# A hybrid decoder block on one core: six split FFN groups, half of SH2 on VectorE, low parts made for two chunks at once

## The chip, the cores and the metric

The kernel runs on one core of one Trainium2 chip. The metric is the device time of one execution in microseconds; a median of several runs stands for a kernel, and one further execution is profiled.

## The reference

One decoder block over 256 tokens of width 2048, all in float32. From a conditioning vector come six vectors (adaLN: shift, scale and gate for each of two halves).

```
mod = silu(c) @ w_ada + b_ada                      # w_ada: 2048 x 12288
sh1, sc1, g1, sh2, sc2, g2 = split(mod, 6)
h = rms_norm(x) * (1 + sc1) + sh1
q, k, v, gb, gc, xt = split(h @ w_in, ...)         # w_in: 2048 x 6144
attn = attention(rms_norm(q), rms_norm(k), v)      # 8 heads of 128, causal
conv = gb * causal_dwconv(gc * xt)                 # 3 taps
x = x + g1 * (concat(rms_norm(attn), rms_norm(conv)) @ w_out)
h2 = rms_norm(x) * (1 + sc2) + sh2
u_gate, u_up = split(causal_dwconv(h2 @ w_ffn_up), 2)   # w_ffn_up: 2048 x 11264
x = x + g2 * ((silu(u_gate) * u_up) @ w_ffn_down)       # w_ffn_down: 5632 x 2048
```

With 256 tokens there is a single attention block, so the selection of past blocks selects nothing.

## The kernel before, in words

**Matmuls in two parts.** TensorE multiplies float32 values that are split in a high part (rounded to the fast format) and a low part (the rest). Each weight tile (128 x 4 x 512) is loaded into a buffer `raw`, ScalarE writes the high part (`split_hi`, L242), VectorE the low part (`split_lo`, L248), and then the next load may start. Activations are split in the same way: a *chunk* is 128 of the 2048 channels for 256 tokens, transposed, with its high half in columns 0 to 255 of a tile and its low half behind. High times high, high times low and low times high are summed in PSUM.

**Slots.** The whole program is one list of slots, written out by hand and by the numbers in `CFG`. A slot uses one weight tile (1 MB; down-projection tiles can be smaller). Slots 0 to 47 are the input projection, in the order of `turns`; slots 48 to 63 the output projection; from slot 64 on come the FFN's segments (`segs`: 8, 5, 5 and 4 groups of 256 gate and 256 up channels), each up-projection followed by its share of the down-projection. While slot i multiplies, the weights of slot i + 2 are split (`la` is 2). All other work is a task put at a slot by `at(...)`; `cls` says whether it stands before (under 2) or behind (2) the split in program order. Each engine runs its instructions in this order. `x_first` and `hi_late` choose, slot by slot, whether the split comes early or late.

**Loads** are issued by SyncE in the order in which they are used, five buffers deep. Each waits until the tile five before it has been used up.

**adaLN.** w_ada is 96 further tiles of 1 MB, fed in between the slots. An entry of `ada` is a piece: part (0 SH1, 1 SC1, 2 G1, 3 SH2, 4 SC2, 5 G2), first chunk, width, whether TensorE sums it, first slot, and how many slots its tiles are spread over. A VectorE piece multiplies each row block by its value of silu(c) and adds (L299). A TensorE piece does the same with matmuls of 32 columns (L293) that hold one PSUM bank until `evac`. `cols` then transposes the sum into columns (L337) and gets A and B, the scale and shift of a chunk; `h_chunks` and `h2_chunks` make the modulated chunks from these, `spread` broadcasts a gate. `fill` is one more TensorE piece, whose tiles lie around `norm2`, the norm between the halves, where TensorE would wait.

**The input projection.** A turn is a tensor (or a pair such as q0, q1) and a range of chunks. Two turns of the same tensor at most two slots apart go on in the same PSUM banks; otherwise `evac_in` empties the banks, the first time with a ScalarE copy (L420), later with a VectorE add (L422). There are eight banks; a pair's turn uses four.

**FFN.** A group takes 4 weight tiles (16 chunks) and 4 banks. In segment 0 the first five groups are done in two turns (`split`: 5 groups, cut at chunk 8): chunks 0 to 7 for all five, then chunks 8 to 15, since the last chunks' scale and shift come late. Each turn ends in `up_sum` (L633, L636; the second adds to the first, L641). `up_conv`, `up_silu` and `up_gate` (L650 to L669) follow at lags set by `up0`. `spill` writes the residual rows to the output to free buffers, `unspill` reads them back.

**Attention and convolution** run beside the input and output projection as tasks (`att_*`, `conv_*`). `mix_tile` splits each of their 16 result chunks; `add_square` sums the squares for the norms. `hold_a` and `evac_out` empty the output projection's banks at the lags `hold` and `evac`.

Of the kernel before, what the change touches and what calls it, by code (L numbers as in the profile page):

```python
# [11 lines left out]
ALU = mybir.AluOpType  # L12
# [19 lines left out]
CFG = {'ada': [[4, 12, 512, False, 62, 10], [3, 0, 512, True, 58, 3], [0, 4, 512, True, 4, 6],  # L32
# [4 lines left out]
 'bufs': [40, 10, 5, 3, 3],  # L37
# [6 lines left out]
 'fill': [[4, 8]],  # L44
 'fill_at': [2, 1, 1],
 'tr3': 0,
 'split': [5, 8],
 'segs': [8, 5, 5, 4],
 'heads': [2, 3, 4, 2, 1, 5, 4, 2],
 'head_steps': [1, 1, 2, 3, 4],  # L50
 'conv': [[1, 2, 2, 5, 3, 6, 7, 8], [2, 3, 3, 3, 2, 3, 2, 6]],
 'qk': [[1, 5], [1, 7]],
 'norms': [50, 55],
 'x1': 55,
 'fcols': 5,
 'vload': 20,
 'spr': [0, 1],
 'slag': [2, 8],
 'sgap': [3, 4],
 'hold': [3, 3, 0],  # L60
 'evac': [4, 1, 1],
 'sq': [7, 5, 2],
 'tr': [7, 6, 2],
 'part': 0,
 'up': [[1, 1, 1], [1, 1, 3], [0, 0, 2], [0, 2, 3]],
 'gate': [-15, -15, -4, -7],
 'cls': {'add': -1,
# [3 lines left out]
         'out_norm': 1,  # L71
         'cols': -1,
         'conv_q': 1,
         'att_q': 0,
         'up_gate': 2,
         'hold_a': 1,
         'spread': 0,
         'conv_m': 2,
         'ffn_cols': -1,
         'h_chunks': 2,  # L80
         'evac_a': 2,
         'evac_down': 2,
         'conv_p': 2,
# [4 lines left out]
         'sq_out': 2,  # L88
         'att_s': -1,
         'tr_out': 1,  # L90
         'evac': 1,
         'qk_stat': 1,
# [3 lines left out]
         'gate_down': 0,  # L96
# [3 lines left out]
         'qk_root': 0,  # L100
         'evac_out': 1,
         'bias': 1,
         'add_bias': 0,
         'up_silu': 2},
 'up0': [[1, 2, 3], [1, 2, 3], [1, 1, 2], [1, 3, 4], [1, 2, 4], [1, 2, 3], [2, 3, 4], [1, 2, 2], [1, 2, 5],
         [1, 2, 8], [0, 1, 3], [1, 3, 3]],
 'la': 2,
 'spill': [6, 6],
 'back': [-27, -27, -10, -22],
 'x_first': [0, 6, 10, 11, 12, 13, 14, 20, 22, 54, 55, 61, 64],  # L110
 'h_act': True,
 'h_lag': 1,
 'hi_late': [0, 1, 3, 4, 5, 8, 9, 10, 12, 15, 19, 27, 31, 32, 40, 42, 45, 48, 50, 52, 54, 55, 59, 63, 65, 70, 71,
# [6 lines left out]
def tile_block(  # L120
# [325 lines left out]
    for i, (fs, k) in enumerate(turns):  # L446
        def near(f, d):
            u = uses[f]
            n = u.index(i) + d
            return 0 <= n < len(u) and abs(u[n] - i) <= 2  # L450

        def go(hi, lo, fs=fs, k=k, new=[not near(f, -1) for f in fs], end=[not near(f, 1) for f in fs]):
            m = 4 // len(fs)
            for h, f in enumerate(fs):
                mm_tok(f, hi[:, h::len(fs)], lo[:, h::len(fs)], [halves(hT[k + j]) for j in range(m)], m, new[h], end[h])
# [99 lines left out]
    for n, (f, part, k) in enumerate(seq):  # L555
        def go(hi, lo, part=part, f=f, k=k, tf=n == len(seq) - 1):
            mm_tok((part, f), hi, lo, [halves(mixT[k + j]) for j in range(4)], 4, k % 8 == 0, k % 8 == 4, tf)
            if k % 8 == 4:
                done.add((part, f))
# [230 lines left out]
    def h_chunks(ks):  # L790
        assert all((part, k) in done for k in ks for part in (SC1, SH1))
        ts = {}
        for n in range(len(ks) + 1):
            if n < len(ks):
                k = ks[n]
                xt = xnT[k // 2][:, (k % 2) * 256:(k % 2) * 256 + 256]
                t = ts[k] = t1k("hf")
                if CFG["h_act"]:
                    act(t, xt, AF.Identity, scale=A1[:, k:k + 1], bias=B1[:, k:k + 1])
                else:  # L800
                    V.tensor_scalar(t, xt, A1[:, k:k + 1], B1[:, k:k + 1], op0=ALU.mult, op1=ALU.add)
                hT[k] = t2k(f"h{k}", F32R)
                act(hT[k][:, :256], t, AF.Copy)  # L803
            if n:
                k = ks[n - 1]
                V.tensor_tensor(out=hT[k][:, 256:], in0=ts[k], in1=hT[k][:, :256].bitcast(F32), op=ALU.subtract)
# [118 lines left out]
    def mix_tile(k, src, gcol):  # L925

        mixT[k] = t2k(f"mix{k}", F32R)
        q, y = t1k("sq"), t1k("my")
        act(y, src, AF.Copy, scale=gcol)
        act(mixT[k][:, :256], y, AF.Copy)  # L930
        act(q, src, AF.Square)
        V.tensor_tensor(out=mixT[k][:, 256:], in0=y, in1=mixT[k][:, :256].bitcast(F32), op=ALU.subtract)
        return q
# [12 lines left out]
    def add_square(w, q, first, last):  # L946
# [5 lines left out]
        if last:  # L952
            p = bank("ss" + w)
            for t in range(2):
                mm(p[:, t:t + 1], sums[w][:, t * P:(t + 1) * P], ones[:, 0:1], start=True, stop=True)
            V.tensor_copy(ssA if w == "A" else ssC, p[:, :2])
# [44 lines left out]
    def conv_c(half, h):  # L1001
        assert f"p{half}" in done
        p = t2k("cp")
        act(p, tr_tok(f"c{half}", h), AF.Copy)
        for k in range(2):
            i = 4 * half + 2 * h + k
            s = p[:, k * 256:(k + 1) * 256]
            y = t1k("cv")
# [5 lines left out]
            cv[i] = y  # L1014

    def conv_g(half, h):
        assert f"g{half}" in done
        done.add(f"gm{half}{h}")
        p = tr_tok(f"g{half}", h)
        for k in range(2):  # L1020
            y = cv[4 * half + 2 * h + k]
            V.tensor_tensor(out=y, in0=p[:, k * 256:(k + 1) * 256], in1=y, op=ALU.mult)

    def conv_m(half, h):
        assert f"gm{half}{h}" in done
        for k in range(2):
            i = 4 * half + 2 * h + k
            cq[i] = mix_tile(8 + i, cv.pop(i), gain["C"][:, i:i + 1])
# [171 lines left out]
```

## Time and profile before

| | |
|---|---|
| median of 3 runs | 1188.88 us (1188.37 to 1189.06) |
| the profiled execution, its own time | 1188.11 us |
| its span | 1186.3 us |
| HBM read / written | 312.77 MB / 4.19 MB |
| granted TensorE clock | 1.00 |

The profile page shows one execution: busy time by engine, the chain of work that ended last, and the costliest groups by source line. Groups can also be listed by form, instructions in order of time, and busy time by stretch. PE is TensorE, PEld its weight loads, DVE VectorE, ACT ScalarE, SP SyncE. Matmuls overlap: one of 512 columns is shown with 0.39 us, while the next begins after 0.23.

### The profile page before, as it was taken

What the parts mean: (1) busy time and instruction counts of PE and PEld (TensorE: products, weight loads), DVE (VectorE), ACT (ScalarE), POOL (GpSimd) and SP (SyncE); (2) the same over time, 40 slices, a digit from 0 to 9 for tenths busy, and PEclk for the clock granted to TensorE, in tenths of its full rate; (3) what the DMA queues carried; (4) which work ended last, traced back from release to release, by engine and by line L of the source; (5) the groups of instructions that cost most, each with busy time, mean ns of one, the idle gap of its engine ahead of it and who ended that gap; (6) DMA issues with size and microseconds to landing.
All of it is one profiled execution on the core that took longest, in us unless ns stands there. A gap on an engine that the chain in (4) does not pass through costs nothing.

```text
span 1186.3 us, 15526 instructions
## 1 busy us (share of the span) xinstructions
PE 1161.6 (98%) x6031; PEld 964.5 (81%) x6031; DVE 917.5 (77%) x1084; ACT 621.0 (52%) x881; POOL 1.2 (0%) x8
## 2 busy tenths in 40 slices
PE   5999999999999999999999999999999999999998
PEld 3767788778878777888888888888888888888886
DVE  3789999978899988778877556998665667576876
ACT  5644356576675365556565443555544455335442
POOL 0000000000000000000000000000000000000000
PEclk9999999999999999999999999999999999999999
DMA  9999999999789999875665787787574655766352
GB/s 361 366 412 368 381 340 331 382 341 329 266 298 337 368 339 320 265 231 178 214 213 180 281 314 286 250 302 266 177 244 154 206 169 196 244 209 212 130 172 89
DMA packets 193277, 317.98 MB, mean 268 GB/s; under 512 B 6922, under 2 KB 106028, under 8 KB 188852
## 3 DMA queue, kind: packets, MB, share of 16 engines
q1 hardware_dynamic: 191876, 314.83, 74.8%
q10 hardware_dynamic: 1328, 2.16, 0.6%
q8 instruction: 47, 0.77, 0.3%
q14 instruction: 26, 0.21, 0.1%
HBM read 312.77 MB, written 4.19 MB: 267 GB/s over the span
## 4 chain that ended last, share of the span: by engine, by line
PE 93%; DVE 4%; DMA 2%; ACT 1%; issue 0%; SPq 0%; DVEq 0%; ACTq 0%
PE z L732 26%; PE z L735 14%; PE ada L293 2%; PE mg L410 1%; PE mk L410 1%; PE mc L410 1%; PE mc L411 1%; PE mg L411 1%; PE mk L411 1%; PE mg L408 1%; PE mc L408 1%; PE mk L408 1%; PE mx L411 1%; PE mx L410 1%; PE mq L410 1%; PE mx L408 1%
## 5 line engine op out<-in xcount | busy, mean ns | idle before, releaser
L248 DVE TENSOR_TENSOR lo<-raw,hi 128x2048 fp32r<-128x2048 f32 (+2 forms) x204 | 448.4, 2204 | 137.6 <-ACT hi L242 127.4
L242 ACT ACTIVATE hi<-raw 128x2048 fp32r<-128x2048 f32 (+2 forms) x204 | 377.1, 1851 | 295.7 <-PE z L732 62.3
L732 PE MATMUL z<-h,hi 128*128 128x512 f32 x1408 | 328.9, 390 | 0.4 <-DVE adaz L339 0.3
L732 PEld LDWEIGHTS z<-h,hi 128*128 128x128 f32 x1408 | 261.3, 188 | 53.3 <-DVE adaz L339 0.8
L735 PEld LDWEIGHTS z<-h,lo 128*128 128x128 f32 x1408 | 175.0, 192 | 3.6
L735 PE MATMUL z<-h,lo 128*128 128x256 f32 x1408 | 176.3, 283 | 0.0
L299 DVE SCALAR_TENSOR_TENSOR ada<-raw,csil,ada 128x512 f32<-128x512 f32 (+3 forms) x150 | 164.1, 1097 | 4.6 <-DMA raw<-in_w_ada_dram 1.3
L636 DVE TENSOR_TENSOR ub<-z,ub 128x256 f32<-128x256 f32 x108 | 38.3, 417 | 42.8 <-ACT ub L633 42.8
L668 ACT ACTIVATE gh<-uy 128x512 fp32r<-128x512 f32 x22 | 13.9, 634 | 78.6 <-DVE uy L666 78.6
L633 ACT ACTIVATE ub<-z 128x256 f32<-128x256 f32 x108 | 32.2, 383 | 26.7 <-PE z L732 26.7
L650 ACT ACTIVATE uy<-ub,fc,fc 128x256 f32<-128x256 f32 x88 | 45.6, 599 | 0.8 <-DVE ub L641 0.8
L657 DVE SCALAR_TENSOR_TENSOR uy<-ub,fc,uy 128x254 f32<-128x254 f32 x88 | 42.5, 483 | 3.1
L655 DVE SCALAR_TENSOR_TENSOR uy<-ub,fc,uy 128x255 f32<-128x255 f32 x88 | 42.1, 479 | 0.0
L293 PE MATMUL ada<-raw,crep 128*32 128x512 f32 (+1 forms) x288 | 33.0, 562 | 8.0 <-DMA raw<-in_w_ada_dram 8.0
L662 ACT ACTIVATE uy<-uy 128x512 f32<-128x512 f32 x22 | 13.9, 630 | 32.3 <-DVE uy L657 32.3
L669 DVE TENSOR_TENSOR gl<-uy,gh 128x512 fp32r<-128x512 f32 x22 | 15.2, 693 | 15.5 <-ACT gh L668 15.5
L410 PE MATMUL mq<-hi,h 128*128 128x512 f32 x64 | 25.4, 397 | 1.6 <-DVE adaz L339 0.8
L410 PE MATMUL mv<-hi,h 128*128 128x512 f32 x64 | 25.5, 398 | 0.9 <-ACT h L803 0.9
L410 PE MATMUL mc<-hi,h 128*128 128x512 f32 x64 | 25.5, 399 | 0.7 <-ACT h L803 0.7
L410 PE MATMUL mg<-hi,h 128*128 128x512 f32 x64 | 25.7, 401 | 0.0
L410 PE MATMUL mk<-hi,h 128*128 128x512 f32 x64 | 25.5, 399 | 0.0
L293 PEld LDWEIGHTS ada<-raw,crep 128*32 128x32 f32 x288 | 7.3, 116 | 22.2 <-issue 10.4
(552 smaller groups left out, 1813.7 us busy)
## 6 DMA issues: line engine op xcount, KB each, us to landing
raw<-in_w_ada_dram SPq DMA_DIRECT2D x96, 1024.0 KB
raw<-in_w_ffn_up_dram SPq DMA_DIRECT2D x176, 512.0 KB
raw<-in_w_in_dram SPq DMA_DIRECT2D x48, 1024.0 KB
raw<-in_w_ffn_down_dram SPq DMA_DIRECT2D x24, 1024.0 KB
raw<-in_w_ffn_down_dram SPq DMA_DIRECT2D x24, 768.0 KB
raw<-in_w_out_dram SPq DMA_DIRECT2D x16, 1024.0 KB
xr<-in_x_dram SPq DMA_DIRECT2D x2, 1024.0 KB
x<-in_x_dram SPq DMA_DIRECT2D x8, 256.0 KB
```

The lines of the kernel that those rows point to most:

```text
L242: act(hi[:, :nk], t[:, :nk], AF.Copy)
L248: V.tensor_tensor(out=lo[:, :nk], in0=t[:, :nk], in1=hi[:, :nk].bitcast(F32), op=ALU.subtract)
L293: mm(self.acc[q:q + 32, :], crep[:, i, :], t[:, j, :], start=(r == 0 and j < 4), stop=(r == self.tiles - 1 and j >= self.rows - 4), tile_p ...
L299: V.scalar_tensor_tensor(out=self.acc, in0=t[:, j, :], scalar=csil[:, i:i + 1], in1=self.acc, op0=ALU.mult, op1=ALU.add)
L408: mm(o, a, lo[:, k, s], start=False, stop=(last and k == nk - 1 and s.stop == 512))
L410: mm(o, a, hi[:, k, s], start=(first and k == 0), stop=False)
L411: mm(o, b, hi[:, k, s], start=False, stop=False)
L650: act(y, b, AF.Identity, bias=fcols[3][:, i:i + 1], scale=fcols[2][:, i:i + 1])
L655: V.scalar_tensor_tensor(out=y[:, 1:], in0=b[:, :255], scalar=fcols[1][:, i:i + 1], in1=y[:, 1:], op0=ALU.mult, op1=ALU.add)
L657: V.scalar_tensor_tensor(out=y[:, 2:], in0=b[:, :254], scalar=fcols[0][:, i:i + 1], in1=y[:, 2:], op0=ALU.mult, op1=ALU.add)
L732: mm(zp[grp][ft], hi[:, j, ft * P:(ft + 1) * P], h2T[k + j], start=begins and j == 0, stop=ends and j == 3)
L735: mm(zp[grp][ft][:, :256], lo[:, j, ft * P:(ft + 1) * P], h2T[k + j][:, :256], start=False, stop=False)
```

## The change

1. adaLN pieces move. SH2's first half, (3,0) and (3,4), is summed by VectorE, no longer by TensorE; the fill is (3,8) instead of (4,8). (0,2) goes to VectorE and (1,2) to TensorE. Last halves of SC2 and SH2, (4,8) and (3,12), come in slots 64 to 72. G2 starts at slot 96 instead of 102, within 19 slots instead of 29.
2. Six FFN groups instead of five go in two turns.
3. The turns of the input projection are in another order; q's chunks 0 to 3 are one stretch.
4. `h_chunks` makes two chunks at once: one copy and one subtraction of 512 columns for a pair (except for the first pair). The convolution's gate, its high and low parts, and its squares are handled two chunks at once in the same way; the last sum of squares then takes four small matmuls instead of two.
5. Buffers: 46 instead of 40 of 2 KB, 6 instead of 10 of 1 KB, 1 instead of 3 of 4 KB.
6. Lags, classes and the lists that place splits early or late get other values.

```diff
-CFG = {'ada': [[4, 12, 512, False, 62, 10], [3, 0, 512, True, 58, 3], [0, 4, 512, True, 4, 6],
-         [2, 0, 2048, False, 28, 22], [5, 0, 2048, False, 102, 29], [1, 8, 1024, False, 7, 15],
-         [3, 8, 512, False, 49, 13], [3, 4, 512, True, 32, 10], [3, 12, 512, False, 51, 13],
-         [0, 8, 512, True, 11, 10], [1, 2, 256, False, 0, 7], [0, 2, 256, True, 0, 7], [4, 4, 512, False, 24, 9],
-         [4, 0, 512, True, 49, 1], [1, 4, 512, False, 3, 6], [0, 12, 512, False, 14, 9]],
- 'bufs': [40, 10, 5, 3, 3],
- 'turns': [['c', 0, 2], ['g', 0, 2], ['k', 0, 2], ['x', 0, 2], ['v', 0, 2], ['q', 0, 2], ['v', 2, 4], ['x', 2, 4],
-           ['k', 2, 4], ['q', 2, 4], ['c', 2, 4], ['g', 2, 4], ['g0', 4, 8], ['x0', 4, 8], ['k0', 4, 8],
...
- 'fill': [[4, 8]],
- 'fill_at': [2, 1, 1],
- 'split': [5, 8],
+CFG = {'ada': [[2, 0, 2048, False, 28, 22], [4, 8, 512, False, 64, 11], [0, 8, 512, True, 11, 10],
+         [0, 4, 512, True, 4, 6], [5, 0, 2048, False, 96, 19], [1, 8, 1024, False, 7, 14],
+         [3, 4, 512, False, 23, 7], [0, 2, 256, False, 2, 2], [1, 2, 256, True, 0, 4], [4, 12, 512, False, 46, 17],
+         [0, 12, 512, False, 15, 7], [1, 4, 512, False, 2, 9], [3, 12, 512, False, 67, 7],
+         [4, 4, 512, False, 34, 13], [3, 0, 512, False, 52, 10], [4, 0, 512, True, 35, 11]],
+ 'bufs': [46, 6, 5, 3, 1],
+ 'turns': [['v', 0, 2], ['c', 0, 2], ['g', 0, 2], ['x', 0, 2], ['k', 0, 2], ['q', 0, 4], ['c', 2, 4], ['x', 2, 4],
+           ['k', 2, 4], ['v', 2, 4], ['g', 2, 4], ['v1', 4, 8], ['g1', 4, 8], ['x0', 4, 8], ['k0', 4, 8],
...
+ 'fill': [[3, 8]],
+ 'fill_at': [2, 5, 8],
+ 'split': [6, 8],
...
- 'hold': [3, 3, 0],
- 'evac': [4, 1, 1],
+ 'hold': [1, 5, 1],
+ 'evac': [2, 4, 0],
...
- 'spill': [6, 6],
+ 'spill': [4, 3],
...
-        ts = {}
-        for n in range(len(ks) + 1):
-            if n < len(ks):
-                k = ks[n]
...
-                hT[k] = t2k(f"h{k}", F32R)
-                act(hT[k][:, :256], t, AF.Copy)
-            if n:
-                k = ks[n - 1]
-                V.tensor_tensor(out=hT[k][:, 256:], in0=ts[k], in1=hT[k][:, :256].bitcast(F32), op=ALU.subtract)
+        for k in ks[::2]:
+            t, hi, lo = t2k("hf"), t2k(f"h{k}", F32R), t2k(f"hl{k}", F32R)
+            two = [slice(j * 256, (j + 1) * 256) for j in range(2)]
+            steps = two if k == 0 else [slice(0, 512)]
+            for j, s in enumerate(two):
+                act(t[:, s], xnT[k // 2][:, s], AF.Identity, scale=A1[:, k + j:k + j + 1], bias=B1[:, k + j:k + j + 1])
+                if k == 0:
+                    act(hi[:, s], t[:, s], AF.Copy)
+                hT[k + j] = hi[:, s], lo[:, s]
+            if k:
+                act(hi, t, AF.Copy)
+            for s in steps:
+                V.tensor_tensor(out=lo[:, s], in0=t[:, s], in1=hi[:, s].bitcast(F32), op=ALU.subtract)
...
+    def conv_m(half, h):
...
+        act(hi, y, AF.Copy)
+        act(c, c, AF.Square)
+        V.tensor_tensor(out=lo, in0=y, in1=hi.bitcast(F32), op=ALU.subtract)
+        cq[half, h] = c
...
-        for j in range(4):
-            add_square("C", cq.pop(4 * half + j), half == 0 and j == 0, half == 1 and j == 3)
+        for h in range(2):
+            add_square("C", cq.pop((half, h)), half == 0 and h == 0, half == 1 and h == 1)
```

More of the change, by code (lines that the diff above doesn't have):

```diff
@@ L87 @@
          'up_sum': 0,
-         'sq_out': 2,
+         'sq_out': 1,
          'att_s': -1,
          'tr_out': 1,
-         'evac': 1,
-         'qk_stat': 1,
+         'evac': -1,
+         'qk_stat': 0,
          'load_x': 0,
@@ L95 @@
          'att_o': 2,
-         'gate_down': 0,
+         'gate_down': 1,
          'conv_g': 0,
@@ L454, in go @@
             for h, f in enumerate(fs):
-                mm_tok(f, hi[:, h::len(fs)], lo[:, h::len(fs)], [halves(hT[k + j]) for j in range(m)], m, new[h], end[h])
+                mm_tok(f, hi[:, h::len(fs)], lo[:, h::len(fs)], [hT[k + j] for j in range(m)], m, new[h], end[h])
         slots.append((pair_load(k, fs[0]) if len(fs) == 2 else w_load(w_in, k, 4, [(COL[fs[0]] * 512, 512)]), 4, go))
@@ L556, in go @@
         def go(hi, lo, part=part, f=f, k=k, tf=n == len(seq) - 1):
-            mm_tok((part, f), hi, lo, [halves(mixT[k + j]) for j in range(4)], 4, k % 8 == 0, k % 8 == 4, tf)
+            mm_tok((part, f), hi, lo, [mixT[k + j] for j in range(4)], 4, k % 8 == 0, k % 8 == 4, tf)
             if k % 8 == 4:
@@ L953, in add_square @@
             p = bank("ss" + w)
+            n = sums[w].shape[1] // 256
             for t in range(2):
-                mm(p[:, t:t + 1], sums[w][:, t * P:(t + 1) * P], ones[:, 0:1], start=True, stop=True)
+                for j in range(n):
+                    a = j * 256 + t * P
+                    mm(p[:, t:t + 1], sums[w][:, a:a + P], ones[:, 0:1], start=j == 0, stop=j == n - 1)
             V.tensor_copy(ssA if w == "A" else ssC, p[:, :2])
@@ L1013, in conv_c @@
                                    op0=ALU.mult, op1=ALU.add)
-            cv[i] = y
+        cv[half, h] = c
     def conv_g(half, h):
```

88 lines of the change are left out of this document (42 added, 46 removed), and 14 rows, old and new, of the table CFG.

## The prediction

> **What bounds the kernel now.** I read the page first, for the engine that carries the chain.
>
> ```profile
> span 1186.3 us, 15526 instructions
> ...
> PE 1161.6 (98%) x6031; PEld 964.5 (81%) x6031; DVE 917.5 (77%) x1084; ACT 621.0 (52%) x881; POOL 1.2 (0%) x8
> ...
> PE 93%; DVE 4%; DMA 2%; ACT 1%; issue 0%; SPq 0%; DVEq 0%; ACTq 0%
> ```
>
> TensorE is busy 1161.6 of 1186.3 us and is 93% of the chain. A saving must therefore take work from TensorE, or remove some of its 24.7 us of idle time. So next I read what TensorE waits for; the columns after the colon are total us, times and longest:
>
> ```profile
> PE ada L293 <- DMA raw<-in_w_ada_dram: 8.0, 3, 6.9
> PE pv_ccol L184 <- DMA vcb<-in_c_dram: 4.6, 1, 4.6
> ...
> PE n2b L592 <- DVE n2d L590: 1.4, 1, 1.4
> PE mv L410 <- ACT h L803: 0.9, 1, 0.9
> PE mq L410 <- DVE adaz L339: 0.8, 1, 0.8
> PE mq L410 <- ACT pa_q L420: 0.8, 1, 0.8
> ```
>
> The first two, 12.6 us, are the first loads, which the change leaves alone. The last three, 2.5 us, lie around the early turns of q. Everywhere else there is hardly anything to win from waits. The third view asks how close VectorE and the DMA stand behind, stage by stage (stretch: length, then busy us of PE, PEld, DVE, ACT, POOL, clock, DMA share, GB/s):
>
> ```profile
> 69.00:167.00 98.00, 98.00 (x459) 75.42 (x460) 95.20 (x104) 40.43 (x51) 0.00 (x0) 1.00 0.98 374
> 167.00:240.00 73.00, 73.00 (x335) 58.83 (x334) 68.52 (x76) 47.17 (x126) 0.00 (x0) 1.00 0.96 358
> 240.00:330.00 90.00, 90.00 (x466) 73.54 (x463) 72.30 (x99) 61.48 (x119) 0.00 (x0) 1.00 0.84 306
> 330.00:442.00 112.00, 110.61 (x543) 84.88 (x542) 102.12 (x139) 63.12 (x104) 0.00 (x0) 1.00 0.94 343
> 449.40:518.00 68.60, 68.25 (x394) 60.10 (x394) 55.22 (x79) 38.00 (x60) 0.00 (x0) 1.00 0.86 288
> 518.00:573.00 55.00, 55.00 (x319) 48.73 (x319) 49.30 (x77) 38.13 (x56) 0.00 (x0) 1.00 0.53 177
> ```
>
> TensorE is full in every stretch, at clock 1.00. But VectorE is at 97% in 69 to 167 us, at 94% in 167 to 240, 80%, 91%, 80% and 90% after that. It is a close second, so work given to it must be placed stretch by stretch.
>
> **SH2's first half leaves TensorE.** Before, six 512-wide adaLN pieces are summed by TensorE (16 rows of weights each, 2 records for each); after, four: (3,0) and (3,4) become VectorE pieces, and the fill is (3,8) instead of (4,8). Two pieces are 8 tiles of 1 MB. What one tile costs is seen on TensorE's timeline (start, us, what) between two turns of the in-projection, and behind the output projection's third group for two tiles in a row:
>
> ```profile
> 225.34 1.97 PE L408 MATMUL mk<-lo,h 128*128 128x512 f32 x8
> 227.25 1.06 PE L293 MATMUL ada<-raw,crep 128*32 128x512 f32 x8
> 228.24 0.50 PE L410 MATMUL mk<-hi,h 128*128 128x512 f32 x1
> 228.58 0.39 PE L411 MATMUL mk<-hi,h 128*128 128x512 f32 x1
> 228.81 0.39 PE L410 MATMUL mk<-hi,h 128*128 128x512 f32 x1
> ...
> 406.00 1.92 PE L293 MATMUL ada<-raw,crep 128*32 128x512 f32 x16
> 407.86 1.12 PE L365 MATMUL adab<-ada,ones 128*128 128x512 f32 x2
> ```
>
> Matmuls start 0.23 us apart (228.58 to 228.81). The eight of L408 need 8 x 0.2275 = 1.82 us, to 227.16; the tile begins 0.09 later, occupies 0.99 (227.25 to 228.24), and the first matmul behind it takes 0.34 instead of 0.23: 1.2 us in all. Two tiles back to back take 1.86 and one switch, 2.1. Of the removed eight, six stand alone and two together: 6 x 1.2 + 2.1 = 9.3 us; with the busy time alone (24.5 us for 192 records, in the next fence) it is 24.5 / 3 = 8.2. I take **-9.3**. The four transposes of a piece into columns stay in both forms.
>
> The price is paid on VectorE. The groups by form (count, then busy us, mean ns of one, idle before):
>
> ```profile
> L248 DVE TENSOR_TENSOR lo<-raw,hi 128x2048 fp32r<-128x2048 f32 x176 | 401.6, 2288 | 114.9 <-ACT hi L242 108.8 <-PE mx L408 3.9 <-DMA raw<-in_w_ffn_up_dram 1.1
> L299 DVE SCALAR_TENSOR_TENSOR ada<-raw,csil,ada 128x512 f32<-128x512 f32 x90 | 67.6, 751 | 3.9 <-DMA raw<-in_w_ada_dram 1.3
> L293 PE MATMUL ada<-raw,crep 128*32 128x512 f32 x192 | 24.5, 602 | 0.5 <-DMA raw<-in_w_ada_dram 0.5
> L636 DVE TENSOR_TENSOR ub<-z,ub 128x256 f32<-128x256 f32 x108 | 38.3, 417 | 42.8 <-ACT ub L633 42.8
> L641 DVE TENSOR_TENSOR ub<-ub,ub 128x512 f32<-128x512 f32 x10 | 6.4, 684 | 0.0
> L806 DVE TENSOR_TENSOR h<-hf,h 128x256 fp32r<-128x256 f32 x16 | 6.3, 423 | 7.1 <-ACT h L803 7.1
> L669 DVE TENSOR_TENSOR gl<-uy,gh 128x512 fp32r<-128x512 f32 x22 | 15.2, 693 | 15.5 <-ACT gh L668 15.5
> L799 ACT ACTIVATE hf<-xnT,B,A 128x256 f32<-128x256 f32 x16 | 9.4, 590 | 1.0 <-DVE B L350 1.0
> L803 ACT ACTIVATE h<-hf 128x256 fp32r<-128x256 f32 x16 | 6.7, 419 | 0.5
> L668 ACT ACTIVATE gh<-uy 128x512 fp32r<-128x512 f32 x22 | 13.9, 634 | 78.6 <-DVE uy L666 78.6
> ```
>
> A piece is 16 x 0.75 = 12 us, so 24 us are added, and where the pieces land counts. In slots 23 to 31 (3,4) takes the place of (4,4): no change. In 34 to 43 (4,4) is new: 12 us in the stretch 240 to 330, where VectorE idles 17.7 us, and TensorE gets (4,0) there in place of (3,4): no change for it. The loads rise by 4 MB, 47 GB/s on 306, below the 374 that the first stretch sustains. In 49 to 63 (3,8) and (3,12) leave, (3,0) and most of (4,12) come: VectorE gets less, the DMA 8 MB less, TensorE the whole saving. Cover holds; without it VectorE would be late by what exceeds its idle, a few us. G2 moves from slots 102 to 129 to 96 to 113, half of it down-projection without convolutions; I cost that at nothing.
>
> **The first FFN turns** carry the rest: in slots 64 to 74 there were three VectorE tiles and now eight ((4,8) and (3,12)), 15 us more, and both must be complete before slot 76, where the second half of the chunks begins; six groups instead of five put that at slot 76 instead of 74. TensorE's timeline, VectorE's, and the chain give the durations (start, us, what; in brackets the idle time before it):
>
> ```profile
> 460.74 0.60 PE L337 MATMUL adac<-ident,adae 128*128 128x128 f32 x4
> ```
>
> ```profile
> 454.71 3.11 DVE L299 SCALAR_TENSOR_TENSOR ada<-raw,csil,ada 128x512 f32<-128x512 f32 x4
> 457.73 4.49 DVE L248 TENSOR_TENSOR lo<-raw,hi 128x2048 fp32r<-128x2048 f32 x2
> ...
> 466.69 0.88 DVE L612 SCALAR_TENSOR_TENSOR h2f<-x1T,A,rB 128x256 f32<-128x256 f32 x2
> ...
> 470.65 2.29 DVE L248 TENSOR_TENSOR lo<-raw,hi 128x2048 fp32r<-128x2048 f32 x1
> ...
> 491.40 0.16 DVE L353 SCALAR_TENSOR_TENSOR adaz<-adaz,vbc 128x4 f32<-128x4 f32 x1 [2.49 <-ACT ada L344]
> ```
>
> ```profile
> 469.44 7.28 PE z L732 x32
> 476.73 3.83 PE z L735 x32
> ```
>
> Time runs from the first z matmul (449.4). VectorE is free at 5.3 (454.71). Until the low part of slot 77 it has 8 tiles x 3.0 = 24, 12 low parts (slots 66 to 77) x 2.24 (two in 4.49) = 27, five groups' sums x 4 x 0.35 = 7.1 (38.3 us for 108), the last eight chunks 2 x 3.96 (466.69 to 470.65) = 7.9, column steps 1, and a wait for ScalarE's sums, 2.5 for one set, for two by my estimate 3.6: 76, and about 77 with a few short waits. TensorE does two slots in 7.28 + 3.83 = 11.1, so with three sets of four transposes (0.6 each) it wants that low part at 13 x 5.55 + 1.8 = 74. The stall is about 3 us; behind it the queue of VectorE holds the next sums, which free the banks, so all later groups shift with it. Bounds: 0, if its short waits overlap better, and 9, half of the 15 + 2.8 us that are added (2.8: the sixth group's second sum, 4 x 0.35 + 2 x 0.68). I take **+3**. The loads rise by 5 MB, 76 GB/s on 288, to 364: still under 374. The four spills come earlier on ScalarE's queue, which has idle time (38.0 of 68.6 us busy).
>
> **q in one stretch, other early steps.** q's two turns become neighbours, so its four banks are emptied once, after both. The two waits of mq are for banks: those of v's unfinished turn, of q and of the adaLN columns fill all eight. That of mv is for h, which stood behind the copies of q's banks on ScalarE. In the new order no turn but q's own is unfinished there, and no copies stand before h: both causes (2.5 us) go. But VectorE at 97% and the DMA at 0.98 set the pace behind: part is given back. I take **-1.5** (0 to -2.5). (0,2) and (1,2) only swap engines; the other turns only change order.
>
> **Two chunks at once.** For a pair the low part is one instruction of 0.69 instead of two of 0.42; with the convolution's products and squares VectorE saves about 3 us, where TensorE doesn't wait for it: 0. But a pair's low half now comes after 2 x 0.59 + 0.63 + 0.69 = 2.5 us instead of 0.59 + 0.42 + 0.42 = 1.4. The Trainium skill, Perfetto Trace Analysis, Optimizing Scalar/DVE Operations, advises breaking instructions up where ScalarE or VectorE aren't saturated yet cause bubbles on others; by it the wait of mv would grow to 2.0 and the sum end 2.6 higher. In 69 to 167 us ScalarE is busy 40.4 of 98, and its h is what mv waited 0.9 us for, so the rule bears on this place; no trace here shows it for pairs.
>
> My sum goes without that growth, since the copies ahead of that h are gone.
>
> **Small rest.** The output projection's second group holds its banks two and then three slots longer (hold 3 to 5, evac 1 to 4), so that around slot 56 three pairs are held when the next group wants its own; that can cost a wait like those above, 0 to 1 us, and I take 0. Fewer small and more 2 KB buffers: attention's q and k halves draw on 6 instead of 10, so ScalarE may wait for the scores, with the low parts two slots ahead; 0. The convolution's last sum gets two more small matmuls, 0.2. Norm2's chain is as long as before: the fill's four tiles now all lie ahead of n2b, none behind: 0.
>
> **Sum.** 1188.1 (the profiled execution) - 9.3 - 1.5 + 3 + 0.2 = 1180.5. The median of the runs, 1188.9, is 0.8 above the profiled one, so about **1181** for the median. About 0.2%, 2.4 us, can be told from no change.
>
> **Rivals.**
> - *VectorE's idle is enough.* No stall in the FFN and the whole 2.5 us early: 1188.9 - 9.3 - 2.5 = 1177. For it: 19 us of idle in 449 to 573 us. Against: most of it is in short waits.
> - *VectorE paces slots 64 to 88.* In 449.4 to 573 us it is busy 104.5 of 123.6; with 18 more, 122.5. A stall of 6 to 9 instead of 3: 1184 to 1187.
> - *Slower.* None of that idle can be used, since it is dependence and not slack: the whole 18 us lands on TensorE in slots 64 to 88, and 1188.9 - 9.3 - 1.5 + 18 = 1196. It decides once the stall exceeds 11 + 2.4 = 13.4 us. Against it: VectorE at 97% in 69 to 167 us with no TensorE wait shows that nearly all its time can be used.
> - *No gain.* Slots 49 to 63 follow VectorE or the DMA (0.94) rather than TensorE, and the removed tiles leave idle time: 1189. Against: both are relieved there as well.
>
> **How the numbers follow.** Forecast 0.5 (1179 to 1183), idle enough 0.17, VectorE paces 0.16, no gain 0.09, slower 0.08. The first three are faster: 0.83, of which I move 0.02 to the neighbours: faster 0.81, same 0.10, slower 0.09. The range goes from 1175.5 (idle enough, with the waits of 330 to 442, 1.4 us, gone) to 1188: the first three cases with the bounds of the stall.
>
> **What would show it.** Right: L293's 512-wide records fall from 192 to 128; L299's 512-wide rise by 30; no mq wait in the first 80 us; TensorE idle of about 3 us between 505 and 520 us, at z with releaser DVE lo or h2's low part; VectorE above 93% there. Wrong: long waits of z for lo through slots 64 to 88; waits for DMA between 200 and 330 us; new waits of w_out's matmuls for banks.

## The result, and the profile after

| | before | after |
|---|---|---|
| median, same chips (13 runs each) | 1188.47 us | 1183.54 us |
| ratio of the medians, 95% interval | | 0.9961 (0.9950 to 0.9971) |
| the profiled execution, its own time | 1188.11 us | 1183.73 us |
| its span | 1186.3 us | 1181.9 us |
| end of the last matmul, from the span's start | 1181.68 us | 1177.30 us |

The change makes the kernel 4.9 us faster, where 7.9 was forecast. 1183.5 us lies in the stated range (1175.5 to 1188) and 0.5 above the 1179 to 1183 of the forecast's own case. The two profiled executions differ by 4.4 us. On the page after, the first lines to read are the busy times: TensorE lost 7.6 us of work, VectorE got 19.7 more.

```profile
span 1181.9 us, 15418 instructions
...
PE 1154.0 (98%) x5971; PEld 963.7 (82%) x5971; DVE 937.2 (79%) x1099; ACT 619.5 (52%) x884; POOL 1.2 (0%) x8
```

TensorE's idle time grew from 24.7 to 27.9 us, so 3.2 of the 7.6 were given back as waits. The waits of TensorE after (total us, times, longest) name them; most lines of the new kernel stand two higher than those of the old (five at the matmuls of the sum of squares). ssA and ssC are the sums of squares of attention and convolution, ap attention's transposes, adaz the reduced columns of an adaLN piece, n2b the broadcast of norm2, z the FFN's up-projection.

```profile
PE ssA L960 <- DVE sq L953: 1.6, 1, 1.6
PE mk L412 <- DVE adaz L341: 1.6, 1, 1.6
...
PE n2b L594 <- DVE n2d L592: 1.4, 1, 1.4
PE z L734 <- DVE h L619: 1.2, 1, 1.2
PE z L734 <- ACT ada L346: 0.9, 2, 0.5
PE mv L412 <- ACT h L802: 0.7, 1, 0.7
PE ap L921 <- ACT s L913: 0.7, 1, 0.7
PE mq L413 <- DVE hl L807: 0.5, 1, 0.5
```

The groups by form show that the work moved as intended: 30 more VectorE sums of 512 columns (90 before), 64 fewer TensorE records (192 before).

```profile
L301 DVE SCALAR_TENSOR_TENSOR ada<-raw,csil,ada 128x512 f32<-128x512 f32 x120 | 89.8, 751 | 3.4
L295 PE MATMUL ada<-raw,crep 128*32 128x512 f32 x128 | 16.4, 602 | 0.0
```

By stretch (length, then busy us of PE, PEld, DVE, ACT, POOL, clock, DMA share, GB/s), VectorE's load rose from 72.3 to 83.1 in 240 to 330 us and from 55.2 to 63.4 in 449 to 518 us, and fell in 330 to 442 us. In 330 to 442 us TensorE's clock is 0.98 and no longer 1.00: there more than waits was lost.

```profile
240.00:330.00 90.00, 89.24 (x462) 70.90 (x461) 83.08 (x115) 59.09 (x121) 0.00 (x0) 1.00 0.95 352
330.00:442.00 112.00, 108.79 (x519) 86.35 (x517) 97.47 (x127) 63.49 (x103) 0.00 (x0) 0.98 0.77 271
449.40:518.00 68.60, 67.66 (x388) 58.87 (x387) 63.42 (x86) 37.67 (x63) 0.00 (x0) 1.00 0.92 321
```

**Where the time went.** Taking the time from each matmul's start to the next, without the waits, and grouping by output tile gives this account of TensorE in the two profiled executions:

| item | before, us | after, us | difference |
|---|---|---|---|
| start of slot 0 | 27.20 | 25.91 | -1.3 |
| adaLN tiles after that | 25.43 | 17.59 | -7.8 |
| matmuls of both projections and of the gates' broadcast (adab), without half clock | 362.3 | 361.6 | -0.7 |
| half clock behind ssA (below) | 0 | 1.6 | +1.6 |
| wait ahead of ssA | 0.71 | 1.60 | +0.9 |
| wait of an adaLN tile ahead of ssA for its load | 0.46 | 0 | -0.5 |
| early waits (mq, mv; then mk, mq) | 2.47 | 2.06 | -0.4 |
| wait of attention's transposes, ap | 0 | 0.76 | +0.8 |
| end of the output projection to the first z | 6.96 | 7.74 | +0.8 |
| waits of z after that | 0.32 | 0.94 | +0.6 |
| small matmuls of ssC | 0.36 | 0.89 | +0.5 |
| attention's matmuls and z | 506.9 | 508.2 | +1.3 |
| rest | | | -0.2 |
| **end of the last matmul** | 1181.68 | 1177.30 | **-4.4** |

(361.6 is from the variant with the late small matmuls, which has no half clock; after itself shows 363.2.) The 0.7 us of the projections and the 1.3 of attention and z I put down to switches between kinds of matmuls, which no run separates; 0.45 of the 1.3 come with the six groups, since z takes that much longer in the kernel before with six groups alone. The gain at the start isn't the change's: 1.2 of it lie in the 32 transposes of x, 5.4 us before and 4.2 after, and among the variants of the kernel after below, where that part is the same, five took 5.4 to 5.9. In the kernel before with six groups slot 0 starts at 25.31 us. The start goes with the clock: in the clock records of the traces the first full clock stands at 21.50 us before and at 15.62 after; over all profiles slot 0 starts at 25.3 to 25.9 us where that is earlier than 17.5, and at 26.6 to 27.8 where it is later than 20.9. Without the start the two profiled executions differ by 3.1 us. The largest unforeseen item is ssA. TensorE's timeline (start, us, what; in brackets the idle time before it):

```profile
345.74 1.02 PE L367 MATMUL adab<-ada,ones 128*128 128x512 f32 x2
348.37 0.58 PE L960 MATMUL ssA<-ones,sq 128*128 128x1 f32 x4 [1.60 <-DVE sq L953]
348.81 1.07 PE L1002 MATMUL trg<-ident,pa_g 128*128 128x128 f32 x8
349.63 0.48 PE L412 MATMUL m('A', 0)0_2877<-hi,mix 128*128 128x512 f32 x1
...
350.23 0.63 PE L412 MATMUL m('A', 0)1_2878<-hi,mix 128*128 128x512 f32 x1
...
352.79 0.63 PE L412 MATMUL m('A', 0)0_2877<-hi,mix 128*128 128x512 f32 x1
353.22 0.54 PE L413 MATMUL m('A', 0)0_2877<-hi,mix 128*128 128x512 f32 x1
353.60 0.40 PE L412 MATMUL m('A', 0)1_2878<-hi,mix 128*128 128x512 f32 x1
```

Four tiny matmuls, whose result can come a slot later (shown below), wait 1.6 us for VectorE, and TensorE, which takes its instructions in order, stands behind them. Then the matmuls start 0.43 us apart until 353.22, where 0.23 is usual: the clock is at half for some 3.4 us. The window shows it too, as a clock of 0.66:

```profile
350.00:355.00 5.00, 5.00 (x17) 3.91 (x16) 4.95 (x8) 4.91 (x11) 0.00 (x0) 0.66 0.01 2
```

Seven intervals of 0.43 us and one of 0.38 instead of 0.23 cost about 1.6 us. The profile before has no such stretch behind the first loads. VectorE is late because the convolution's taps, four from 345.53 on, stand ahead of the sum in its queue; the last of them and the sum:

```profile
346.95 0.48 DVE L1016 SCALAR_TENSOR_TENSOR cv<-cp,v1c,cv 128x254 f32<-128x254 f32 x1
347.35 0.88 DVE L953 TENSOR_TENSOR sq<-sq 128x256 f32<-128x256 f32 x2
```

### The profile page after: what moved, and what is told of

Same layout as the page of the kernel before. It is cut to its first block, busy times and chain, and to the rows that moved or that the text cites. A ratio compares the mean times of both kernels' runs of the same rounds, so it can differ in the third digit from the quotient of the medians.

```text
span 1181.9 us, 15418 instructions
## 1 busy us (share of the span) xinstructions
PE 1154.0 (98%) x5971; PEld 963.7 (82%) x5971; DVE 937.2 (79%) x1099; ACT 619.5 (52%) x884; POOL 1.2 (0%) x8
## 4 chain that ended last, share of the span: by engine, by line
PE 57%; DVE 0%; issue 0%
PE z L734 24%; PE z L737 13%; PE m('D', 0, 3)0_5847 L410 0%; PE m('D', 0, 3)1_5848 L413 0%; PE m('D', 0, 3)0_5847 L413 0%; PE m('D', 0, 3)0_5847 L412 0%; PE m('D', 0, 2)0_5812 L410 0%; PE m('D', 0, 2)1_5813 L413 0%; PE m('D', 0, 2)0_5812 L413 0%; PE m('D', 0, 2)0_5812 L412 0%; PE m('D', 0, 1)0_5568 L410 0%; PE m('D', 0, 1)1_5569 L413 0%; PE m('D', 0, 1)0_5568 L413 0%; PE m('D', 0, 1)0_5568 L412 0%; PE m('D', 0, 0)0_5518 L410 0%; PE m('D', 0, 0)1_5519 L413 0%
## 5 line engine op out<-in xcount | busy, mean ns | idle before, releaser
L301 DVE SCALAR_TENSOR_TENSOR ada<-raw,csil,ada 128x512 f32<-128x512 f32 (+3 forms) x180 | 186.4, 1039 | 4.2
L635 ACT ACTIVATE ub<-z 128x256 f32<-128x256 f32 x112 | 33.5, 386 | 27.8 <-PE z L734 27.8
L295 PE MATMUL ada<-raw,crep 128*32 128x512 f32 (+1 forms) x224 | 24.3, 539 | 8.4 <-DMA raw<-in_w_ada_dram 8.2
L412 PE MATMUL mk<-hi,h 128*128 128x512 f32 x64 | 25.3, 396 | 1.6 <-DVE adaz L341 1.6
L412 PE MATMUL mx<-hi,h 128*128 128x512 f32 x64 | 25.7, 401 | 0.0
L413 PE MATMUL mq<-hi,hl 128*128 128x512 f32 x64 | 25.1, 392 | 0.5 <-DVE hl L807 0.5
L412 PE MATMUL mq<-hi,h 128*128 128x512 f32 x64 | 25.3, 396 | 0.0
```

The lines of the kernel that those rows point to most:

```text
L301: V.scalar_tensor_tensor(out=self.acc, in0=t[:, j, :], scalar=csil[:, i:i + 1], in1=self.acc, op0=ALU.mult, op1=ALU.add)
L412: mm(o, a, hi[:, k, s], start=(first and k == 0), stop=False)
L413: mm(o, b, hi[:, k, s], start=False, stop=False)
L635: act(c[ft // 2][:, (ft % 2) * 256:(ft % 2) * 256 + 256], zp[grp][ft][:, 256:], AF.Copy)
```

## The experiments

Each was measured beside the kernel before, on the same chip; the ratio is to that. "After" alone, repeated, gave 0.9966 (0.9953 to 0.9978).

| kernel | median, us | ratio, 95% interval |
|---|---|---|
| after, repeated | 1183.38 | 0.9966 (0.9953 to 0.9978) |
| after, all of SH2's first half back on TensorE | 1199.41 | 1.0099 (1.0085 to 1.0113) |
| after, (3,4) alone back on TensorE | 1188.09 | 1.0006 (0.9997 to 1.0014) |
| before, SH2's first half on VectorE | 1199.54 | 1.0103 (1.0089 to 1.0117) |
| before, six groups in two turns | 1190.24 | 1.0018 (1.0010 to 1.0027) |
| after, h one chunk at a time | 1184.15 | 0.9968 (0.9957 to 0.9978) |
| after, sum of squares and add a slot later | 1187.50 | 1.0001 (0.9992 to 1.0010) |
| after, only the small matmuls a slot later | 1180.04 | 0.9936 (0.9925 to 0.9948) |
| that, and (4,8) from slot 62 | 1184.22 | 0.9970 (0.9959 to 0.9981) |
| that, and (3,0) from slot 50 | 1184.37 | 0.9969 (0.9957 to 0.9981) |
| both of these | 1187.03 | 0.9994 (0.9985 to 1.0003) |
| only the small matmuls later, (1,2) in three slots | 1179.68 | 0.9927 (0.9914 to 0.9941) |

**The kernel after, again.** Is the half clock part of the kernel or an accident?

> The changed kernel unaltered. Two theories on its half clock (0.5 for 3.4 us behind the wait for the sum of squares, matmuls 0.43 instead of 0.23 us apart, about 1.7 us lost). Theory A, it belongs to this order of work: the profile shows it again at the same place, the idle time is again near 28 us, and the median stays near 1183.5. Theory B, it falls as the clock's windows happen to lie: it is missing here, and this profiled execution is about 1.7 us shorter than the first one.

Neither theory held as it was put. The span was 1182.2 us and most waits were the same, ssA's 1.6 among them, but the half clock came at 288 us, behind a wait of ap that was 1.6 us instead of 0.7, and not behind ssA. So a stretch recurs, and the same wait of ssA is followed by one in one execution and not in the next. What decides between them is the last section's subject.

**SH2's first half back on TensorE**, in the kernel after.

```diff
-         [3, 4, 512, False, 23, 7], ... [3, 0, 512, False, 52, 10], ...
+         [3, 4, 512, True, 23, 7], ... [3, 0, 512, True, 52, 10], ...
```

> The changed kernel with only the two SH2 pieces back on TensorE, in their new slots. Theory 1, the SH2 move is more than the whole gain and everything else in the change costs: 8 tiles come back, 8.4 to 9.3 us, so about 1192, slower than before. Rival, VectorE paces the changed kernel and hides much of the saving: relieved of 24 us it gives back waits, and the time is 1185 to 1188.

It cost 16 us, more than either expectation. In the profiled execution the adaLN tiles after the start took 8.0 us more, the projections' matmuls beside them about 1.8, and slot 0 started 1.3 later, which is no part of it; most of the rest is waits that did not exist in the kernel before. On TensorE's timeline the largest is for a bank of the output projection's third pair:

```profile
401.16 0.79 PE L412 MATMUL m('A', 2)1_3301<-hi,mix 128*128 128x512 f32 x1 [4.15 <-DVE y L509]
```

A TensorE piece occupies one bank from its first tile to its last, here slots 52 to 61, and the longer holds of the new output projection need that bank; with (3,0) on VectorE the same pair waits 0.2 us. A stretch at half clock comes with the 4.15 us, but none follows ssA here, so that the clock adds nothing to the 16.

**(3,4) alone back on TensorE**, to see the price of a piece that meets no shortage of banks.

```diff
-         [3, 4, 512, False, 23, 7],
+         [3, 4, 512, True, 23, 7],
```

> The changed kernel with only the piece (3,4), slots 23 to 28, back on TensorE; (3,0) stays on VectorE. Theory 1, of the 16 us that both pieces cost when they went back, 8.8 to 9.7 are tiles and 4.8 are waits for banks, since (3,0) holds one in slots 52 to 59, where the output projection's groups hold theirs longer now: here 4.4 to 4.9 us slower than the changed kernel, 1188 to 1189, and no wait of the third group for banks. Rival, banks play no part and each piece costs half of the 16 us: 1191 to 1192.

The first theory was right: 4.7 us by the two medians, where the prediction's price of 1.2 us a tile makes 4.8, and no wait of the third pair beyond its 0.2. In the trace the tiles' own time rose by 4.0, and that of q's and k's matmuls beside them by 1.0. A piece that meets no shortage of banks is worth its tiles, switches included, and no more.

**SH2's first half on VectorE in the kernel before**, with nothing else changed.

```diff
-         ... [3, 0, 512, True, 58, 3], ... [3, 4, 512, True, 32, 10], ...
+         ... [3, 0, 512, False, 58, 3], ... [3, 4, 512, False, 32, 10], ...
```

> The kernel before with only the two SH2 pieces moved to VectorE, in their old slots (32 to 39 and 58 to 60). Theory 1, VectorE's idle time covers them: 1188.5 - 9 = about 1179.5, better than the whole change. Rival, placing counts: four tiles in slots 58 to 60 make the low parts late before norm2, with a TensorE wait of 3 to 6 us there: 1183 to 1186.

Both missed: it is 12 us slower than the kernel before on the same chip. The tiles' own time falls by 7.8 us, but TensorE's waits show how late VectorE now comes:

```profile
PE adac L337 <- DVE ada L299: 6.3, 3, 2.4
...
PE n2b L592 <- DVE n2d L590: 3.3, 1, 3.3
```

On VectorE's own timeline three tiles in a row stand ahead of everything else, and further such runs follow at 425 and 430 us:

```profile
409.94 0.47 DVE L297 TENSOR_SCALAR ada<-raw,csil 128x512 f32<-128x512 f32 x1
410.44 8.50 DVE L299 SCALAR_TENSOR_TENSOR ada<-raw,csil,ada 128x512 f32<-128x512 f32 x11
```

(3,0) has only three slots there, its columns are wanted at once, and four stretches at half clock come on top. Taking the tiles off TensorE is worth less than nothing in the old places. The 16 us between this kernel and the one after are the rest of the change; that the new places are most of them is likely from these waits, but no run moved the places alone.

**Six groups alone**, in the kernel before.

```diff
- 'split': [5, 8],
+ 'split': [6, 8],
```

> The kernel before with six instead of five groups in two turns, nothing else. Theory 1, the sixth group's second sum (2.8 us of VectorE, 1.5 of ScalarE) lies in idle time: within 1 us of before, no new TensorE wait between 500 and 600 us. Rival, VectorE paces the second turns, where the low parts were already late by 0.9 us in slot 86: 2 to 4 us slower.

The rival was right: 0.18% slower, 2.6 us by the medians. The wait it foresaw is for low parts in the second turns:

```profile
PE z L735 <- DVE lo L248: 2.1, 2, 1.7
```

So more groups in two turns have a cost of their own on VectorE; in the kernel after this wait does not appear.

**h one chunk at a time**, in the kernel after (the old loop of `h_chunks` put back, the convolution left in pairs).

> The changed kernel with h made one chunk at a time as before; the convolution stays in pairs. Theory 1, pairs only pay where VectorE is late: the 0.5 us wait for the pair's low part in the sixth turn shrinks or goes, and the time is within 1 us of the changed kernel. Rival, pairs free VectorE and ScalarE at slots 22 and 23, where the low parts have no lead left: without them new waits, 1 to 3 us slower.

The first theory was right: the intervals of the ratios nearly coincide. The wait of mq fell from 0.5 to 0.2 us, which is what the pair costs there; a gain from pairs elsewhere is not to be seen above the noise.

**The sum of squares a slot later**, matmuls and add together.

```diff
- 'head_steps': [1, 1, 2, 3, 4],
+ 'head_steps': [1, 1, 2, 3, 5],
- 'norms': [50, 56],
+ 'norms': [51, 56],
```

> The changed kernel with the heads' sums of squares added one slot later, so that TensorE finds the last sum ready (the norm one slot later too). Theory 1, that wait (1.6 us) and the half clock that follows it are lost time: the wait is gone, the clock is 1.00 throughout, and the time is 1.6 to 3.3 us under the changed kernel's. Rival, the wait only moves to another place or the norm's readers become late: no change within 1 us, and a new wait at the output projection's first banks.

Both missed: the wait grew from 1.6 to 5.2 us, and the kernel lost its whole gain.

```profile
PE ssA L960 <- DVE sq L953: 5.2, 1, 5.2
```

A slot later does not mean with more room: VectorE now does a tile's four sums ahead of the add, and TensorE still waits at the next place in its queue.

```profile
354.07 3.10 DVE L301 SCALAR_TENSOR_TENSOR ada<-raw,csil,ada 128x512 f32<-128x512 f32 x4
...
357.70 0.86 DVE L953 TENSOR_TENSOR sq<-sq 128x256 f32<-128x256 f32 x2
```

**Only the small matmuls a slot later.** The add stays in slot 50, the four matmuls and the copy go to slot 51.

```diff
+            def finish():
+                p = bank("ss" + w)
+                ...
+            if w == "A":
+                late.append(finish)
...
+        if w == "A":
+            late.pop()()
- 'norms': [50, 56],
+ 'norms': [51, 56],
```

> The changed kernel with the heads' squares added in their old slot, but the small matmuls that sum them over the channels (and the norm) one slot later, so that VectorE's order in front of the sum stays and TensorE asks later. Theory 1, TensorE stood in its own queue behind one small matmul: the 1.6 us wait goes, nothing takes its place, and with one half-clock window less the time is 1.6 to 3.3 us below the changed kernel's 1183.5: 1180 to 1182. Rival, the norm is then too late for the output projection's banks: a wait of like size at the second or third group, and 1183 to 1185.

The first theory was right: 3.3 us faster than after by the medians, and the intervals do not meet. On TensorE's timeline the sum has no bracket, and the window that showed 0.66 shows 1.00; no other stretch at half clock came in its place.

```profile
352.69 0.50 PE L962 MATMUL ssA<-ones,sq 128*128 128x1 f32 x4
```

```profile
350.00:355.00 5.00, 5.00 (x25) 4.17 (x24) 4.96 (x7) 4.48 (x8) 0.00 (x0) 1.00 0.42 145
```

So a wait of 1.6 us had cost about 1.6 + 1.6.

**Two attempts around norm2 and slot 74**, on top of that kernel.

```diff
- [4, 8, 512, False, 64, 11]
+ [4, 8, 512, False, 62, 11]
```

> The kernel with the late output sum, and (4,8) starting at slot 62 instead of 64, so that its sixteen tiles end two slots before those of (3,12) and its columns are made at another slot. Theory: the two waits of z for ScalarE's copies of the column sets (0.32 and 0.53 us around 501 us) come because two sets want banks at once; apart they go, 0.5 to 0.9 us less than the late sum alone: 1179.2 to 1179.6. Rival: two more VectorE tiles come before norm2, where VectorE is already late (its lead is -0.66 us at slot 62), and TensorE waits there for the low part of slot 62 or 63: 1 to 3 us more, 1181 to 1183.

```diff
- [3, 0, 512, False, 52, 10]
+ [3, 0, 512, False, 50, 10]
```

> The kernel with the late output sum, and (3,0) starting at slot 50 instead of 52, so that its last VectorE tiles and its columns lie two slots further ahead of norm2. Theory: norm2 starts late since VectorE still works off adaLN tiles when the last output matmuls end; with the room the wait of z for the second low half (1.2 us) stays, but the evacuation starts on time: 0.5 to 0.9 us less, 1179.1 to 1179.5. Rival: the tiles only move to slots 50 to 52, where the convolution's last sums and the squares of the output lie; the wait for the sum of squares comes back there: 1 to 2 us more.

> Both moves: (4,8) from slot 62 and (3,0) from slot 50. Theory: the two add up, 1178.0 to 1179.0. Rival: what one move takes from VectorE ahead of norm2 the other puts back, and it stays at 1180 within 0.5.

All three theories fell. The first two cost 4.2 and 4.3 us by the medians, more than their rivals said, though by the rivals' mechanism; both together cost 7.0, where neither side expected a loss. In the first, VectorE's timeline ahead of norm2 has one tile more, in front of the low part and of the last evacuation:

```profile
428.78 0.48 DVE L299 TENSOR_SCALAR ada<-raw,csil 128x512 f32<-128x512 f32 x1
429.30 2.33 DVE L301 SCALAR_TENSOR_TENSOR ada<-raw,csil,ada 128x512 f32<-128x512 f32 x3
431.54 2.29 DVE L250 TENSOR_TENSOR lo<-raw,hi 128x2048 fp32r<-128x2048 f32 x1
```

Without the move that low part starts at 428.80. The 2.75 us arrive whole: z starts 3.3 us later, and slot 65 4.4, with the half clock that follows. The tile costs its full price because VectorE sets the time from the last output matmul to z. The waits of z for the column sets stayed (1.1 us): they are no fight for one bank at one time. In the second, the sums of the earlier tiles stand on VectorE ahead of the copy of attention's sum of squares and of the convolution's last addition:

```profile
PE adab L367 <- DVE ssA L963: 1.5, 1, 1.5
...
PE ssC L962 <- DVE cv L953: 1.2, 1, 1.2
```

**(1,2) in three slots**, on top of the kernel with the late small matmuls.

```diff
- [1, 2, 256, True, 0, 4]
+ [1, 2, 256, True, 0, 3]
```

> The kernel with the late output sum, and (1,2), the small TensorE piece at the start, spread over three slots instead of four, so that the reduction of its columns stands on VectorE ahead of a low part and of the eight sums of (0,2) (2.3 and 4.1 us), no longer behind them. Theory: the wait of mk for that reduction (1.57 us at slot 4) is a wait for the columns' bank, held while VectorE works off (0,2); with the reduction early it goes, and 1.6 us less remain at the end: 1178.4. Rival: VectorE at 97% and the DMA at 0.98 set the pace of 69 to 167 us, where the low parts are ready 0.7 us behind to 0.5 us ahead of their slots at slots 20 to 26; TensorE comes there 1.6 us earlier, waits for low parts, and most of it is given back: 1179.5 to 1180.

VectorE's timeline shows the reduction now ahead of the low part and of the eight sums of (0,2):

```profile
49.08 0.16 DVE L341 TENSOR_REDUCE adaz<-adac 128x2 f32<-128x8 f32 x1
...
51.76 4.12 DVE L301 SCALAR_TENSOR_TENSOR ada<-raw,csil,ada 128x256 f32<-128x256 f32 x8
```

The wait of mk is gone, which shows its cause, and the last matmul ends 1.4 us earlier in the profiled execution (span 1176.8). The medians, 1179.68 and 1180.04, are too close to tell apart, and the first lies where the rival put it: the trace speaks for the theory, the times do not decide. This is the fastest version run: 8.5 us under the kernel before on its chip.

## Why the prediction was right, and which of its steps were not

**The tiles, -9.3.** Right, a little too large: 7.8 us of the tiles themselves and 0.7 of switches beside them, 8.5 together, between the bound of 8.2 and the value taken; the 0.7 is what all moves together left, and not measured by itself. One piece put back cost 4.7 where the step says 4.8. What the step lacked is that a TensorE piece also holds a bank: both pieces put back cost 16 us.

**Cover in the slots where the tiles land.** The statement that VectorE has room in 34 to 63 held for the sum of busy time, and not for order: ap's new wait (0.8 us) and ssA's growth (0.9 us) are VectorE or what follows it coming late in 280 to 350 us. For ssA the taps were shown above; the scores for ap come from ScalarE, which waits 2.3 us for VectorE's maxima (until 283.05), and these stand behind five sums of G1, 5.4 us from 276.86 on. Calling the cover "a few us" if it failed was the right size for this, and far too little for the same pieces in their old places, which cost 12 us instead of gaining 9.

**q in one stretch, -1.5.** This step failed: 0.4 us instead. The banks and h no longer make mq and mv wait, but the claim that both causes go overlooked that the columns of (1,2), now a TensorE piece, take a bank in just that place. VectorE empties it behind 4.1 us of (0,2)'s sums. The two timelines after, first TensorE's and then VectorE's:

```profile
50.60 0.38 PE L339 MATMUL adac<-ident,adae 128*128 128x128 f32 x2
...
55.76 0.50 PE L412 MATMUL mk<-hi,h 128*128 128x512 f32 x1 [1.58 <-DVE adaz L341]
```

```profile
51.50 4.13 DVE L301 SCALAR_TENSOR_TENSOR ada<-raw,csil,ada 128x256 f32<-128x256 f32 x8
55.54 0.16 DVE L341 TENSOR_REDUCE adaz<-adac 128x2 f32<-128x8 f32 x1
```

"(0,2) and (1,2) only swap engines" was the sentence that cost it: a swap of engines also swaps who holds a bank. The rest of the wait, 0.5 us at mq for a pair's low half, is the pair itself.

**The FFN turns, +3.** The mechanism did not act. Slot 77's low part starts at 515.28 and is done at 517.6, 74.2 us after the first z (443.36), where 77 was reckoned. Slot 77 starts at 518.9, in the middle of the 32 low matmuls below, 75.5 us after the first z, where 74 was reckoned.

```profile
515.28 2.29 DVE L250 TENSOR_TENSOR lo<-raw,hi 128x2048 fp32r<-128x2048 f32 x1
```

```profile
516.98 4.00 PE L737 MATMUL z<-h,lo 128*128 128x256 f32 x32
```

1.3 us of room are left, and VectorE is busy 63.4 of 68.6 us, 92%. VectorE is free at 448.61, 5.3 us after the first z, as reckoned. From there to 517.57 its timeline has 22.9 us of tiles for the 24 of the sum, 26.5 of low parts for 27, 6.8 of sums for 7.1, 7.4 of chunks for 7.9. The wait for ScalarE's column sums, put at 3.6 for two sets, is 0.6, but the short waits, put at about 1, are 3.9. So the waits together were sized right by luck, and the 2.8 us by which VectorE was early are nearly all tiles and parts that were each put a little high. TensorE, for its part, lost time there: z waits twice for ScalarE to empty the column sets.

```profile
501.75 0.50 PE L734 MATMUL z<-h,hi 128*128 128x512 f32 x1 [0.32 <-ACT ada L346]
502.78 3.25 PE L734 MATMUL z<-h,hi 128*128 128x512 f32 x13 [0.53 <-ACT ada L346]
```

That is 0.9 us, 0.6 more than z waited before, against the 3 of the sum; the lower bound 0 was nearer. In the kernel before with six groups the low parts do make z wait, 2.1 us, at later groups: the mechanism exists, and in the kernel after it stays 1.3 us away at slot 77.

**Two chunks at once, 0.** Right: with single chunks the ratio is 0.9968 against 0.9966. The rule of the Trainium skill (Perfetto Trace Analysis, Optimizing Scalar/DVE Operations) that smaller instructions may let work finish sooner holds here by 0.25 us at mq, not by the 2.6 that it would have made; the wait of h moved to mq and did not grow with the pair's length.

**Small rest.** Banks at slot 56: 0.2 us, which the kernel before has too, so nothing, as taken. ssC's matmuls 0.5 for 0.2. Norm2 was put at nothing and cost 0.8: from n2b to z both kernels take 2.7 us, but from the last output matmul to n2b it is 5.0 instead of 4.2 (440.64 - 435.62, and 446.72 - 442.49). VectorE reaches the evacuation late, and a low part of 2.3 us stands ahead of it. TensorE's timelines, before and then after:

```profile
442.49 2.78 PE L293 MATMUL ada<-raw,crep 128*32 128x512 f32 x24
446.72 0.67 PE L592 MATMUL n2b<-n2d,ones 128*128 128x256 f32 x2 [1.45 <-DVE n2d L590]
```

```profile
435.62 3.64 PE L295 MATMUL ada<-raw,crep 128*32 128x512 f32 x32
440.64 0.67 PE L594 MATMUL n2b<-n2d,ones 128*128 128x256 f32 x2 [1.38 <-DVE n2d L592]
```

G2 at nothing was right: no wait of TensorE in 640 to 720 us, at a DMA share of 0.97.

**What no step had:** ssA's wait, the half clock behind it and ap's wait, together +3.3, less 0.5 for a load's wait that went. Against the sum's -7.6, the profiled executions differ by 4.4. The 3.2 us between are these 2.8, 1.1 at q, 0.8 at the tiles, 0.8 at norm2 and 0.3 at ssC, less the 2.4 us of an FFN stall that did not come; the start's -1.3, which is no part of the change, and 1.3 of switches cancel, and 0.2 is the rest. So it was luck that the forecast lay closer than its steps: the overpriced stall covered for 2.4 of some 5.8 us that were missed.

**The signs.** Of those named for being right, the records of TensorE and VectorE came out (192 to 128, and 30 more). The stall between 505 and 520 us did not, VectorE is at 91% there and not above 93%, and mq still waits, 0.5 us at 67.1. None of the signs of being wrong came.

**Rivals.** "VectorE's idle is enough" was right for the FFN and wrong elsewhere. "No gain" named the right stretch, slots 49 to 63, but there only 2.5 us, wait and clock at ssA, came back. That VectorE paces slots 64 to 88, and that all 18 us land on TensorE, did not happen.

## What to carry to other kernels

Work taken off the bounding engine is worth its time only with a place for it in the other engine's order: moving the same two pieces gained 16 us in one arrangement and lost 12 in the other. When a piece changes engine, list the banks it frees or takes beside its instructions. Look for small instructions that stand in the bounding engine's queue ahead of large ones though nobody needs them yet: moving four tiny matmuls behind a slot's work gained 3.3 us, while moving their input with them lost 4.1.

## What the runs showed of the hardware

A stretch of half clock, some 3.4 us long, came with TensorE waits of only 1.2 to 1.9 us: behind ssA (1.60), behind ap (1.65 and 1.93), behind ssC (1.18). The one at ssA cost 1.6 us. Not every such wait has one. mk's 1.58 us at 55.76 has none in any of these profiles, and the same 1.60 us of ssA has one in two profiles (after, and h one chunk at a time) and none in three (after again, and the two kernels with pieces back on TensorE).

The clock records of the traces show what differs between executions. In all fourteen profiles the clock changes only at whole steps of 3.41 us from its first full stretch: in after that begins at 15.62 us, the half clock 98 steps later at 350.12, and the full clock one step later at 353.54. In the kernel before with SH2's half on VectorE, half clock begins at 245.90, 293.68, 419.98 and 437.04 us, which are 14, 37 and 5 steps apart. Where the steps lie differs from one execution to the next: the first full stretch begins between 15.06 and 23.27 us. In after, ssA's wait (346.77 to 348.37) lies whole in the step before the half clock, 346.71 to 350.12, and small sums and transposes fill most of the rest: only 0.5 us of that step are full matmuls. In after again a step ends at 349.82, in the middle of the wait (349.00 to 350.60), each of the two steps has 1.4 us of full matmuls or more, and no half clock follows.

A wait that lies whole in one step is not enough: mk's 1.58 us does so in after (53.16 to 56.58), with 1.8 us of full matmuls around it. So what surrounds the wait counts as well. The Trainium skill (TensorE: Matmul & The Clock Gate, Part 1: The HAM clock gate) has the clock fall after an idle window of about 3.4 us that runs freely: the length of the steps and their changing position agree, the idle time that is needed does not, unless light work counts as idle. By its Part 4 (PE-mode transpose) transposes don't count as busy in the same way, which fits these places; no run here separated transposes from waits, so this stays open.
